# A Strassen down projection with five running sums per output block, and another staging place for the last up tiles

## The chip, the cores and the metric

The kernel runs on one core of one Trainium2 chip. The metric is the device time of one execution in microseconds (us); lower is better. Three executions of the kernel before took 2719.97, 2726.58 and 2727.91 us, median 2726.58. The profiled execution took 2729.51 us; its records span 2727.7 us.

The engines are named as in the profile: PE is TensorE's matmuls (PEld its weight loads), DVE is VectorE, ACT is ScalarE, POOL is GpSimd and SP is SyncE, on which all the transfers spoken of here are issued. Each engine works through its own instructions in a fixed order; semaphores hold an instruction back until what it needs is done.

## The reference

The reference is one inference step of a two-layer decoder over 1024 prompt tokens and 64 sample tokens, which the kernel treats as one matrix of T = 1088 columns. Layer 0 mixes with a state-space model, layer 1 with attention over a cache; each then has the same kind of MLP, and that is the part that matters here:

```python
def sqrelu_mlp(x, w_up, w_down):
    h = jax.nn.relu(x @ w_up)
    return (h * h) @ w_down
...
h = h + sqrelu_mlp(rmsnorm(h, p["norm_mlp"][i]), p["w_up"][i], p["w_down"][i])
```

D_MODEL is 1024 and the hidden width 4096. All is float32.

## The kernel before, in words

**Arithmetic.** A float32 operand is kept as a high and a low part, and one product of two operands is three matmuls (`mm3`, whose matmul is line 209). Making the two parts is `split`: an ACT copy (line 221) and a DVE subtraction (line 222).

**Tiling.** T is cut into four chunks of CN = 272 columns. Activations lie transposed: features on the 128 partitions, tokens along the free axis. A product of 2x2 blocks is done with seven block products in place of eight (Strassen's scheme in Winograd's form). `weight_ops` (lines 390 to 425) loads a raw weight tile, forms the seven weight operands with four POOL instructions (lines 416, 417, 418 and 422) and splits them; `operands` does the same for activations.

**`seven`** (lines 427 to 454) runs the seven products p0 to p6 of one output unit and makes the four quarters c11, c12, c21, c22 from them. Each product goes to one of three pairs of PSUM banks, taken in turn, so p(i+3) cannot start before p(i) has been read. The scheme is: s1 = p0 (ACT copy, line 439); u2 = p1 + s1 (DVE, 441); c11 = p2 + s1; u4 = p3 + u2 (DVE, 445); c22 = p4 + u4; u2 = p4 + u2 (DVE, 449); c12 = p5 + u4; c21 = p6 + u2. In the up stage a product is 24 matmuls, in the down stage 12.

**`mlp`** first runs 16 up tiles (14, 0 to 13, 15). The hidden rows are eight blocks b of two tiles; for b = 0 to 6 `to_hidden` turns a pair of tiles into seven activation operands and stores them in DRAM (`hops`). The rows of block 7 (tiles 14 and 15) are not combined: their four quarters are split in four staging places of `setA` (`hl4`) and stored in `hcnv`, eight stores, two for each quarter. The stores and the loads of the next operands share SP's queue and are chained one after the other (`load_on`, issue on line 526).

**The down stage** (lines 609 to 646) works on an array `H5` that is `setA` seen as two column groups by two halves n by eight output row blocks. For each hidden block b = 0 to 6 and each half d of the output rows it has a *pair* of units, e = 0 and e = 1; while the e = 1 unit of a pair runs, the weight operands of the next pair are made. So there are 28 units in a layer, of 84 matmuls each. `out` adds a quarter into H5. For b = 0 it writes H5 (one DVE instruction, line 627). For b = 1 to 6 it takes a DVE addition of the PSUM bank (line 629) and a POOL addition of s1, u4 or u2 (line 630): seven DVE, one ACT and four POOL instructions in a unit. For b = 1 to 4 POOL also adds the residual that was saved before the MLP (line 646), two instructions in a unit. Two tiles of H5 matter for the start: rows 0 to 3 (d = 0) of the half n = 1, into which c12 and c22 go, lie in the first 1088 words of `setA[1]` and `setA[3]`, and the fourth staging place is the first 1088 words of `setA[1]`. The first staging place is the first 1088 words of `setA[0]`, where c11 and c21 of d = 0 go. For b = 0 and d = 0 the two units run by turns, product by product.

**Block 7** is then multiplied plainly, without the seven products (lines 647 to 666).

**Order.** The program is written in its natural order, and a scheduler (`schedule_with_timeline_sim=True`) fixes the order in which each engine gets its instructions. The order therefore changes where the program does, on every engine.

## Time and profile before

| what | value |
|---|---|
| median of three runs | 2726.58 us (2719.97 to 2727.91) |
| profiled execution | 2729.51 us, span 2727.7 us, mean granted TensorE clock 0.978 |
| busy, whole span | PE 2564.0 us (94%), DVE 1959.2 (72%), ACT 1256.6 (46%), POOL 1213.1 (44%) |
| matmuls of 128 x 272 (line 209, three largest groups) | 15800, of 20369 matmuls in all |
| down-stage additions | line 629 DVE x192, line 630 POOL x192 |

The down stage of layer 0 begins on PE at 843.32 us and block 7 near 1167 us; in layer 1 the same steps lie some 1498 us later (2341.55 us). PE is 94% busy, so the times that matter are the short stretches where it isn't, and what PE waits for there. Busy times of the other engines count only where PE waits for them.

### The profile page before, as it was taken

How to read it: one execution, taken by the hardware profiler on the slowest of the kernel's cores; microseconds unless marked ns; L12 is line 12 of the kernel's file. 1: busy time of each engine (PE TensorE's matmuls, PEld its weight loads, DVE VectorE, ACT ScalarE, POOL GpSimd, SP SyncE). 2: the span in 40 equal slices, each digit the busy share in tenths (PEclk: the TensorE clock that was granted, in tenths of full speed). 3: DMA queues.
4: the chain of work that ended last, by engine and by line, in shares of the span. 5: the costliest groups of instructions: out<-in, count | busy, mean ns of one | idle time of the engine just before them, and what ended most of it. 6: DMA issues, size and time to landing. Idle time of an engine off the chain costs nothing.

```text
span 2727.7 us, 54053 instructions
## 1 busy us (share of the span) xinstructions
PE 2564.0 (94%) x20369; PEld 2392.2 (88%) x20369; DVE 1959.2 (72%) x3406; ACT 1256.6 (46%) x2612; POOL 1213.1 (44%) x1119
## 2 busy tenths in 40 slices
PE   6888899999998999999999999999989999899998
PEld 5777779899998999999889867777989999899998
DVE  8898665988886777794323278886588788677776
ACT  5433444566663222244322367775366665322224
POOL 4576310323321799842310455651032222179984
PEclk8999899999999999999999999999999999999999
DMA  6445352266558567443476889986226656866741
GB/s 200 106 104 146 117 163 76 91 242 243 229 228 324 232 254 277 178 167 102 150 259 222 268 290 308 304 294 218 91 87 244 236 227 234 318 242 244 285 169 67
DMA packets 242283, 561.66 MB, mean 206 GB/s; under 512 B 54053, under 2 KB 129382, under 8 KB 224614
## 3 DMA queue, kind: packets, MB, share of 16 engines
q1 hardware_dynamic: 212646, 548.50, 56.7%
q10 hardware_dynamic: 28864, 8.92, 1.4%
q8 instruction: 161, 2.64, 0.4%
q0 software_dynamic: 512, 0.79, 0.1%
q14 instruction: 100, 0.82, 0.1%
HBM read 386.19 MB, written 171.93 MB: 205 GB/s over the span
## 4 chain that ended last, share of the span: by engine, by line
PE 41%; DVE 18%; POOL 10%; DMA 10%; issue 6%; ACT 4%; SPq 0%; POOLq 0%; ACTq 0%; DVEq 0%
PE banks L209 39%; DMA hops<-plain 5%; DVE rounded L222 5%; POOL plain L630 4%; DVE plain L222 4%; PE banks L1667 1%; POOL plain L416 1%; DMA rounded<-hmid 1%; DVE plain L578 1%; POOL plain L646 1%; ACT plain L221 1%; POOL plain L422 1%; DMA hcnv<-plain 1%; POOL plain L417 1%; DMA plain<-fpast 1%
## 5 line engine op out<-in xcount | busy, mean ns | idle before, releaser
L209 PE MATMUL banks<-rounded 128*128 128x272 f32 (+3 forms) x11168 | 1552.6, 295 | 72.8 <-ACT rounded L221 18.3
L209 PEld LDWEIGHTS banks<-rounded 128*128 128x128 f32 x11168 | 1456.7, 191 | 120.3 <-ACT rounded L221 21.1
L221 ACT ACTIVATE rounded<-plain 128x512 fp32r<-128x512 f32 (+5 forms) x573 | 379.8, 676 | 637.5 <-PE banks L209 449.3
L222 DVE TENSOR_TENSOR rounded<-plain,rounded 128x512 fp32r<-128x512 f32 (+4 forms) x518 | 502.8, 976 | 121.7 <-ACT rounded L221 120.3
L209 PE MATMUL banks<-mlp,rounded 128*128 128x272 f32 x3816 | 516.8, 290 | 12.2 <-DVE plain L627 4.8
L209 PEld LDWEIGHTS banks<-mlp,rounded 128*128 128x128 f32 x3816 | 493.8, 189 | 17.2 <-DVE plain L627 5.3
L416 POOL TENSOR_TENSOR plain<-plain 128x512 f32<-128x512 f32 x60 | 103.9, 1731 | 705.9 <-DVE rounded L222 705.9
L630 POOL TENSOR_TENSOR plain<-plain,flex 128x544 f32<-128x544 f32 x192 | 289.8, 1520 | 37.7 <-DVE plain L629 34.8
L222 DVE TENSOR_TENSOR plain<-plain 128x544 fp32r<-128x544 f32 x212 | 171.1, 820 | 69.9 <-ACT plain L221 69.1
L221 ACT ACTIVATE plain<-plain 128x544 fp32r<-128x544 f32 x212 | 136.7, 650 | 111.6 <-DMA hops<-plain 99.1
L629 DVE TENSOR_TENSOR plain<-banks,plain 128x544 f32<-128x544 f32 x192 | 137.9, 718 | 50.3 <-PE banks L209 46.8
L422 POOL TENSOR_TENSOR plain<-plain 128x512 f32<-128x512 f32 x60 | 98.3, 1639 | 63.0 <-DVE rounded L222 62.6
L209 PE MATMUL banks<-flexr,rounded 128*128 128x272 f32 x816 | 114.5, 290 | 4.0 <-DVE flexr L222 4.0
L209 PE MATMUL banks<-layer 128*32 128x256 f32 (+3 forms) x1152 | 111.9, 368 | 5.5 <-DVE layer L1770 1.7
L579 ACT ACTIVATE plain<-plain 128x544 f32<-128x544 f32 (+1 forms) x136 | 83.2, 613 | 66.0 <-DVE plain L578 65.5
L209 PEld LDWEIGHTS banks<-flexr,rounded 128*128 128x128 f32 x816 | 107.8, 191 | 4.4 <-DVE flexr L222 4.4
L222 POOL TENSOR_TENSOR rounded<-plain,rounded 64x512 fp32r<-64x512 f32 (+2 forms) x55 | 77.9, 1424 | 67.1 <-ACT rounded L221 61.9
L222 POOL TENSOR_TENSOR rounded<-flex,rounded 128x544 fp32r<-128x544 f32 (+7 forms) x100 | 65.9, 668 | 83.7 <-ACT rounded L221 71.0
L578 DVE TENSOR_TENSOR plain<-banks,plain 128x544 f32<-128x544 f32 (+1 forms) x136 | 90.5, 666 | 11.8 <-PE banks L209 11.2
L222 DVE TENSOR_TENSOR rounded<-banks,rounded 128x512 fp32r<-128x512 f32 (+2 forms) x136 | 86.0, 637 | 13.1 <-ACT rounded L221 11.3
L221 ACT ACTIVATE rounded<-banks 128x512 fp32r<-128x512 f32 (+2 forms) x136 | 75.1, 559 | 42.0 <-PE banks L1667 29.3
L418 POOL TENSOR_TENSOR plain<-plain 128x512 f32<-128x512 f32 x60 | 91.7, 1528 | 2.8
(365 smaller groups left out, 3227.0 us busy)
## 6 DMA issues: line engine op xcount, KB each, us to landing
hops<-plain SPq DMA_DIRECT2D x196, 544.0 KB
rounded<-hops SPq DMA_DIRECT2D x66, 1088.0 KB
plain<-in_cache_kT SPq DMA_DIRECT2D x128, 384.0 KB
layer<-in_cache_v SPq DMA_DIRECT2D x128, 384.0 KB
mlp<-hops SPq DMA_DIRECT2D x32, 1088.0 KB
plain<-in_w_up SPq DMA_DIRECT2D x32, 1024.0 KB
plain<-in_w_down SPq DMA_DIRECT2D x28, 1024.0 KB
plain<-in_xT SPq DMA_DIRECT2D x8, 1088.0 KB
```

The source lines that it names most:

```text
L209: PE.matmul(out, a, b, start=first, stop=last)
L221: S.activation(H, src, AF.Copy)
L222: return e.tensor_tensor(L, src, H.bitcast(F32), op=ALU.subtract)
L416: G.tensor_tensor(a22, a21, a22, op=ALU.add)
L417: G.tensor_tensor(a21, a11, a21, op=ALU.subtract)
L418: G.tensor_tensor(a11, a22, a11, op=ALU.subtract)
L422: G.tensor_tensor(a12, a12, a11, op=ALU.subtract)
L578: V.tensor_tensor(x, ps, u, op=ALU.add)
L579: S.activation(x, x, AF.Relu)
L629: V.tensor_tensor(h, ps, h, op=ALU.add)
L630: G.tensor_tensor(h, h, u, op=ALU.add)
L646: G.tensor_tensor(hc, hc, hr[:, m, :], op=ALU.add)
```

## The change

Names: in the lists below `banks` is PSUM, `flex_8251` the area that holds the temporaries, `plain` the area that holds `setA` (so H5) and the raw weights, `rounded` the split operands.

The down stage no longer uses `seven`. The function that runs one product is taken out of it (`products`), and the down stage keeps, for each unit, five sums over all b: the four quarters in H5 and a fifth one, u2 (`sums2`). For b = 0 they are written, and for later b added to:

- p0 goes into c11 and u2, p3 into c12 and c22, p4 into c22 and c21 (two places each); p1 goes into u2, p2 into c11, p5 into c12, p6 into c21.
- A product that goes to two places is copied from PSUM by ACT to a temporary and added to the one place by DVE, straight from PSUM, and from the temporary to the other by POOL (`twice`, and the three lines after p4). For b = 0 the ACT copy writes the first place itself, and DVE's `once` for the following product reads that place as its second operand.
- At b = 6 u2 is added to c22, c12 and c21 on POOL, three instructions in a unit.
- A unit with b = 1 to 5 now has seven DVE, three ACT and three POOL instructions, with b = 6 seven, three and six, and with b = 0 five, three and none. Over both layers POOL additions go from 192 to 168, ACT copies from 56 to 168, DVE additions from 392 to 376.
- `sums2` lies in the first 2176 words of `flex`, and five temporaries of 544 words behind it.

The fourth staging place moves from words 0 to 1087 of `setA[1]` to words 1088 to 2175, which in H5 are rows 4 to 7, so d = 1.

```diff
-    def seven(lhs, rhs, nk, gs, tmp, out):
-
-        s1, u2, u4 = (t[:, gs] for t in tmp)
-
+    def products(lhs, rhs, nk, gs):
         def product(i):
...
+        return product
...
-                hl4 = [hl.p[1], hl.p[0], hl.p[2], setA[1].sub(0, 1088)]
+                hl4 = [hl.p[1], hl.p[0], hl.p[2], setA[1].sub(1088, 1088)]
...
-        small = joined([sq0, rs0])
-        tmps = Ring([small.sub(544 * i, 544) for i in range(6)])
+
+        sums2 = Place(flex.t, 0, SET // 4).at([128, 2, 4, CN])
+        tmps = Ring([Place(flex.t, SET // 4 + 544 * i, SET // 4 + 544 * i + 544) for i in range(5)])
...
-                    def out(m, n, ps, u):
-                        h = H5[:, :, n, 4 * d + 2 * e + m, :]
+                    m0 = 4 * d + 2 * e
+                    c11, c12, c21, c22 = (H5[:, :, n, m0 + m, :] for m in range(2) for n in range(2))
+                    u2 = sums2[:, :, 2 * d + e, :]
...
+                    def twice(a, c, ps):
+
                         if b == 0:
-                            V.tensor_tensor(h, ps, u, op=ALU.add)
+                            S.activation(a, ps, AF.Copy)
                             return
-                        V.tensor_tensor(h, ps, h, op=ALU.add)
-                        G.tensor_tensor(h, h, u, op=ALU.add)
...
+                        t = tmps(sh)
+                        S.activation(t, ps, AF.Copy)
+                        V.tensor_tensor(a, ps, a, op=ALU.add)
+                        G.tensor_tensor(c, c, t, op=ALU.add)
+
+                    def once(a, ps, c=None):
+                        V.tensor_tensor(a, ps, a if c is None or b else c, op=ALU.add)
+
+                    twice(c11, u2, product(0))
+                    yield
+                    once(u2, product(1), c11)
+                    yield
+                    once(c11, product(2))
+                    yield
+                    twice(c12, c22, product(3))
+                    yield
+                    ps = product(4)
+                    once(c22, ps, c12)
+                    if b == 0:
+                        S.activation(c21, ps, AF.Copy)
+                    else:
+                        t = tmps(sh)
+                        S.activation(t, ps, AF.Copy)
+                        G.tensor_tensor(c21, c21, t, op=ALU.add)
+                    yield
+                    if b == 6:
+                        G.tensor_tensor(c22, c22, u2, op=ALU.add)
+                    once(c12, product(5))
+                    yield
+                    once(c21, product(6))
+                    if b == 6:
+                        for c in (c12, c21):
+                            G.tensor_tensor(c, c, u2, op=ALU.add)
+                    yield
```

Below, lines of the changed kernel carry its own numbers: `twice` is lines 634 to 642 (637 the b = 0 copy, 640 the copy, 641 DVE, 642 POOL), `once` is line 645, p4's copy is 658 (b = 0) or 661, POOL's addition to c21 is 662, and the additions of u2 at b = 6 are 665 and 671.

**The start of the down stage.** DVE before, from the first two writes of H5 on (line 627 writes c11, then c22 and later quarters of the d = 0 units; 445 and 449 are u4 and u2; a DMAHW wait is one for a transfer):

```order
L627 TENSOR_TENSOR plain<-banks,flex_8251 128x2x272 [waits DMAHW7_49,DVE_49]
L627 TENSOR_TENSOR plain<-banks,flex_8251 128x2x272 [waits DMAHW0_49]
L445 TENSOR_TENSOR flex_8251<-banks,flex_8251 128x544 [waits PE_49]
L222 TENSOR_TENSOR rounded<-plain,rounded 128x512 [waits Activation_49]
L222 TENSOR_TENSOR rounded<-plain,rounded 128x512 [waits PE_49,Activation_49]
L627 TENSOR_TENSOR plain<-banks,flex_8251 128x2x272 [waits DMAHW0_49,DVE_49]
L449 TENSOR_TENSOR flex_8251<-banks,flex_8251 128x544
```

After, the first writes of H5 are ACT's copies of p0, behind the last splits of the staging, and the first DVE rows are these two pieces:

```order
L637 ACTIVATE plain<-banks 128x2x272 [waits DMAHW7_49]
L637 ACTIVATE plain<-banks 128x2x272 [waits DMAHW0_49,PE_49]
```

```order
L645 TENSOR_TENSOR flex_8251<-banks,plain 128x2x272 [waits PE_49,Activation_49]
L645 TENSOR_TENSOR flex_8251<-banks,plain 128x2x272 [waits DVE_49,PE_49,Activation_49]
L222 TENSOR_TENSOR rounded<-plain,rounded 128x512 [waits Activation_49]
L645 TENSOR_TENSOR plain<-banks,plain 128x2x272 [waits DMAHW7_49,DVE_49,PE_49]
L645 TENSOR_TENSOR plain<-banks,plain 128x2x272 [waits DMAHW0_49,DVE_49,PE_49]
L222 TENSOR_TENSOR rounded<-plain,rounded 128x512 [waits Activation_49]
L222 TENSOR_TENSOR rounded<-plain,rounded 128x512 [waits PE_49,Activation_49]
L645 TENSOR_TENSOR plain<-banks,plain 128x2x272 [waits PE_49]
```

The third line-627 row, which waits for a transfer and stands ahead of line 449, has no counterpart after: the rows that follow c11 there wait for PE and ACT only.

**POOL in a unit that makes weights**, b = 5, d = 0, e = 1. Before, and then after:

```order
L416 TENSOR_TENSOR plain<-plain 128x4x128
L417 TENSOR_TENSOR plain<-plain 128x4x128
L630 TENSOR_TENSOR plain<-plain,flex_8251 128x2x272
L418 TENSOR_TENSOR plain<-plain 128x4x128
L630 TENSOR_TENSOR plain<-plain,flex_8251 128x2x272
L422 TENSOR_TENSOR plain<-plain 128x4x128
```

```order
L642 TENSOR_TENSOR flex_8251<-flex_8251 128x2x272 [waits Activation_49]
L416 TENSOR_TENSOR plain<-plain 128x4x128 [waits DMAHW6_49,DVE_49]
L417 TENSOR_TENSOR plain<-plain 128x4x128 [waits Pool_49]
L418 TENSOR_TENSOR plain<-plain 128x4x128 [waits Pool_49]
L642 TENSOR_TENSOR plain<-plain,flex_8251 128x2x272 [waits Activation_49]
L422 TENSOR_TENSOR plain<-plain 128x4x128 [waits DVE_49,Pool_49]
L662 TENSOR_TENSOR plain<-plain,flex_8251 128x2x272 [waits Activation_49]
```

The addition to u2 now stands ahead of the first weight instruction, and the addition between 417 and 418 is gone.

**DVE in the same unit, after**: each `once` behind a POOL addition waits for POOL, and `twice`'s addition waits for ACT's copy of the same bank. Before, none of the additions to H5 or the temporaries waited for POOL's addition to another quarter of the same unit.

```order
L641 TENSOR_TENSOR plain<-banks,plain 128x2x272 [waits Activation_49]
L645 TENSOR_TENSOR flex_8251<-banks,flex_8251 128x2x272 [waits PE_49,Pool_49]
L645 TENSOR_TENSOR plain<-banks,plain 128x2x272 [waits DVE_49,PE_49]
L222 TENSOR_TENSOR rounded<-plain,rounded 128x512 [waits Activation_49]
L222 TENSOR_TENSOR rounded<-plain,rounded 128x512 [waits PE_49,Activation_49]
L641 TENSOR_TENSOR plain<-banks,plain 128x2x272 [waits Activation_49]
L222 TENSOR_TENSOR rounded<-plain,rounded 128x512 [waits PE_49,Activation_49]
L645 TENSOR_TENSOR plain<-banks,plain 128x2x272 [waits DVE_49,PE_49]
L222 TENSOR_TENSOR rounded<-plain,rounded 128x512 [waits Activation_49]
L645 TENSOR_TENSOR plain<-banks,plain 128x2x272 [waits Pool_49]
```

The three rows with POOL or ACT in their wait (641, 645 on u2 and the last 645, on c22) are the new links; ACT's copy of p4 (line 661) in turn waits for that last DVE row.

More of the change, by code (lines that the diff above doesn't have):

```diff
@@ L437, in product, with seven @@
             return v[:, gs]
+        return product
+    def seven(lhs, rhs, nk, gs, tmp, out):
+        s1, u2, u4 = (t[:, gs] for t in tmp)
+        product = products(lhs, rhs, nk, gs)
         S.activation(s1, product(0), AF.Copy)
@@ L623, in down @@
                 def down(e):
-                    def out(m, n, ps, u):
-                        h = H5[:, :, n, 4 * d + 2 * e + m, :]
+                    m0 = 4 * d + 2 * e
+                    c11, c12, c21, c22 = (H5[:, :, n, m0 + m, :] for m in range(2) for n in range(2))
+                    u2 = sums2[:, :, 2 * d + e, :]
+                    product = products(lambda i, k: (W[i][:, 0, e, k, :], W[i][:, 1, e, k, :]),
+                                       lambda i, g, k: tuple(ops[i][:, k, x, CN * g:CN * g + CN] for x in range(2)),
+                                       2, slice(0, 2))
```

3 lines of the change are left out of this document (removed).

## The prediction

> **What bounds the kernel now.** I read the page first (PE is 94% busy, so only its gaps count), then a table of stretches over the down stage of layer 0. Its columns are length, PE, PEld, DVE, ACT and POOL busy, granted clock, and transfers.
>
> ```profile
> 816.00:884.00 68.00, 56.32 (x412) 55.16 (x411) 42.83 (x61) 26.44 (x45) 12.11 (x8) 0.92 0.88 333
> 884.00:952.00 68.00, 67.05 (x534) 66.61 (x533) 49.99 (x65) 16.36 (x27) 50.14 (x37) 1.00 0.56 217
> 952.00:1020.00 68.00, 63.90 (x497) 62.34 (x496) 50.85 (x63) 16.03 (x27) 63.38 (x47) 1.00 0.66 258
> 1020.00:1088.00 68.00, 65.76 (x516) 64.67 (x516) 51.21 (x65) 16.16 (x27) 65.54 (x49) 1.00 0.70 273
> 1088.00:1156.00 68.00, 67.50 (x531) 66.46 (x530) 54.34 (x66) 16.82 (x27) 57.83 (x40) 1.00 0.50 197
> ```
>
> Two places lose time: the first stretch (PE 56.32 of 68, POOL hardly used), and the third and fourth, where POOL is busy 63.38 and 65.54 of 68. The first, on PE's timeline and then on DVE's, ACT's and SP's, with the last row from the chain of waits:
>
> ```profile
> 843.32 3.27 PE L209 MATMUL banks<-rounded 128*128 128x272 f32 x24 [0.94 <-DVE plain L449]
> 853.52 1.76 PE L209 MATMUL banks<-mlp,rounded 128*128 128x272 f32 x12 [0.93 <-DVE flex L441]
> 857.71 3.09 PE L209 MATMUL banks<-mlp,rounded 128*128 128x272 f32 x12 [2.42 <-DVE plain L627]
> 861.47 4.74 PE L209 MATMUL banks<-rounded 128*128 128x272 f32 x36 [0.67 <-DMA rounded<-hops]
> 872.93 9.24 PE L209 MATMUL banks<-rounded 128*128 128x272 f32 x53 [6.72 <-DVE flex L449]
> 856.95 1.39 DVE L627 TENSOR_TENSOR plain<-banks,flex 128x544 f32<-128x544 f32 x2
> 871.52 0.72 DVE L627 TENSOR_TENSOR plain<-banks,flex 128x544 f32<-128x544 f32 x1 [5.54 <-DMA hcnv<-plain]
> 880.08 0.72 DVE L627 TENSOR_TENSOR plain<-banks,flex 128x544 f32<-128x544 f32 x1 [0.78 <-PE banks L209]
> 848.82 2.29 ACT L221 ACTIVATE plain<-plain 128x544 fp32r<-128x544 f32 x4
> 851.14 4.43 SPq L526 DMA_DIRECT2D hcnv<-plain  x2
> 857.16 6.60 SPq L526 DMA_DIRECT2D hcnv<-plain  x5
> 860.04 11.39 DMA hcnv<-plain
> 2371.28 10.16 PE L209 MATMUL banks<-rounded 128*128 128x272 f32 x60 [6.79 <-DVE flex L449]
> ```
>
> PE stands still for 6.72 us because DVE's write of c22 at 871.52 waits for a store of `hcnv` that lands at 871.43: the fourth staging place is where it writes. Layer 1 shows the same gap (6.79). The clean rate of PE comes from a run without gaps and the row behind it:
>
> ```profile
> 1024.08 9.18 PE L209 MATMUL banks<-rounded 128*128 128x272 f32 x72
> 1033.09 1.16 PE L209 MATMUL banks<-mlp,rounded 128*128 128x272 f32 x8
> ```
>
> 72 matmuls take 1033.09 - 1024.08 = 9.01 us, 0.1251 each: 1.50 us a product, 10.5 a unit, 21.02 a pair. The first pair of the stage starts at 843.32 and its last quarter is evicted from 880.08, 36.8 us later where 21.0 would do. The other losses I read off DVE's additions for p1 of the e = 0 units, one pair apart where I name pairs:
>
> ```profile
> 904.15 0.72 DVE L441 TENSOR_TENSOR flex<-banks,flex 128x544 f32<-128x544 f32 x1 [0.30 <-PE banks L209]
> 1085.43 0.71 DVE L441 TENSOR_TENSOR flex<-banks,flex 128x544 f32<-128x544 f32 x1
> 1107.30 0.71 DVE L441 TENSOR_TENSOR flex<-banks,flex 128x544 f32<-128x544 f32 x1
> ```
>
> The eight pairs of b = 1 to 4 take 181.28 us, 22.66 each, so 1.64 over the clean 21.02. The first pair of b = 5, which has no residual additions, takes 21.87: 0.85 over. So POOL matters in b = 1 to 4, and what is left in b = 5 is waiting between engines.
>
> **What the move of the staging place is worth.** It removes the wait of 871.52: c12 and c22 of d = 0 no longer touch a staged place. What stays is the first staging place, under c11 and c21. Its new first writer is ACT's copy of p0, behind ACT's four staging splits, which end at 848.82 + 2.29 = 851.1. The store of its high half was issued at 851.14 and both halves had landed by 856.95, where DVE wrote c11. In the changed order DVE does its staging splits without line 441 between them, so I put the second store at about 853.1 and its landing at 855.5 (nearest row: the second store went on SP before 855.57 = 851.14 + 4.43, and c11 was free 1.4 us later). Then p1 of e = 1, which needs p0's bank, starts near 854.3, and p2 near 856.2, in place of 853.52 and 857.71, and nothing later in the pair waits for a store: of the 84 x 2 = 168 matmuls the remaining 120 take 15.0 us, and 871.2 is the end of the pair. The slow clock after a gap (0.92 in this stretch; the 53 matmuls at 872.93 would take 6.63 at 0.1251 and took 9.24, 2.6 more) may stay: 873.8. Against 880.08 that is 6.3 us a layer; I take 6.2, with 2 (ACT's copies are held as long as DVE's line 627 was, and p4 is late) to 9 (no slow clock either) as bounds.
>
> The Trainium skill, "TensorE: Matmul & The Clock Gate", part 1, says that a window without matmuls drops PE's clock and that it takes some time of work to come back. The trace agrees in the slow 53 matmuls after the 6.72 us gap. By it the shorter gaps after the change would cost less of this than 2.6.
>
> **What the five sums cost in a steady unit.** First the throughput. Groups by line, and one e = 1 unit of b = 5 on POOL, DVE and ACT:
>
> ```profile
> L630 POOL TENSOR_TENSOR plain<-plain,flex 128x544 f32<-128x544 f32 x192 | 289.8, 1520 | 37.7 <-DVE plain L629 34.8
> L629 DVE TENSOR_TENSOR plain<-banks,plain 128x544 f32<-128x544 f32 x192 | 137.9, 718 | 50.3 <-PE banks L209 46.8
> L439 ACT ACTIVATE flex<-banks 128x544 f32<-128x544 f32 x25 | 15.3, 612 | 7.1 <-PE banks L209 5.4 <-ACT rounded L221 1.7
> 1094.11 1.29 POOL L416 TENSOR_TENSOR plain<-plain 128x512 f32<-128x512 f32 x1 [0.63 <-DVE rounded L222]
> 1095.48 1.29 POOL L417 TENSOR_TENSOR plain<-plain 128x512 f32<-128x512 f32 x1
> 1096.73 1.81 POOL L630 TENSOR_TENSOR plain<-plain,flex 128x544 f32<-128x544 f32 x1
> 1098.51 1.75 POOL L418 TENSOR_TENSOR plain<-plain 128x512 f32<-128x512 f32 x1
> 1100.21 1.38 POOL L630 TENSOR_TENSOR plain<-plain,flex 128x544 f32<-128x544 f32 x1
> 1101.55 1.74 POOL L422 TENSOR_TENSOR plain<-plain 128x512 f32<-128x512 f32 x1
> 1103.24 3.59 POOL L630 TENSOR_TENSOR plain<-plain,flex 128x544 f32<-128x544 f32 x2
> 1103.76 0.71 DVE L629 TENSOR_TENSOR plain<-banks,plain 128x544 f32<-128x544 f32 x1
> 1104.39 2.99 DVE L222 TENSOR_TENSOR rounded<-plain,rounded 128x512 fp32r<-128x512 f32 x2
> 1103.86 0.61 ACT L439 ACTIVATE flex<-banks 128x544 f32<-128x544 f32 x1
> ```
>
> A pair had 8 POOL additions and has 6: 2 x 1.4 = 2.8 us of POOL fall away (1.38 and 1.81 are the ends). POOL was busy some 63.38/68 x 22.66 = 21.1 to 65.54/68 x 22.66 = 21.8 us of a pair; 18.3 to 19.0 is left, under PE's 21.02. As a throughput bound POOL is gone. ACT gains four copies of 0.61 a pair, some 2.4 us on an engine that was 16.16 busy of 68; DVE keeps 14 additions of 0.72.
>
> Then the waits. The new chain in an e = 1 unit is p3, ACT's copy, POOL's addition to c22, DVE's addition of p4, ACT's copy of p4, POOL's addition to c21, DVE's addition of p6; POOL also does the weight instructions there, in the order u2, 416, 417, 418, c22, 422, c21. I lay it on the clock of the quoted unit:
>
> - POOL adds to u2 from 1093.6 (p0's copy, in the place of line 439) to 1095.0, and 416, 417, 418 follow, to 1099.3 (1.29, 1.29 and 1.75).
> - c22 += p3's copy ends between 1100.7 (1.38) and 1101.1 (1.81). DVE, in its order, first finishes the splits ahead of it; c22 += p4 ends near 1102.9 to 1103.2.
> - 422 ends at 1102.4 to 1102.9, so ACT's copy of p4 stands behind ACT's split of its result and ends at 1103.7 to 1104.3; only then is p4's bank free. The changed PE order starts the next unit with p1 instead of p0, and p1 waits for a weight split at 1102.2 to 1102.5.
> - c21 += p4's copy ends at 1105.1 to 1106.5 and DVE's c21 += p6 is done at 1105.8 to 1107.2; the unit's last bank pair would be wanted at about 1104.4.
>
> So PE loses 1.3 to 2.5 us at each such unit; the e = 0 units make no weights, POOL has 3 x 1.4 us of work in 10.5 there, and I cost them at nothing (cover: the third bank pair; without it each POOL link is 1.4). I take 1.8, nearer the low end, since of the POOL rows above 416, 417 and one 630 stand at 1.29 to 1.38. Against before:
>
> - b = 1 to 4: 8 x (1.8 - 1.64) = +1.3 (bounds -2.7 and +6.9).
> - b = 5: 1.2 a pair, without residual additions, against 0.85 in the first pair: two pairs, +0.7 (-0.5 to +2).
> - b = 6: three more POOL additions a unit, two of e = 0 ahead of 416 and two between 417 and 422: 422 moves back by up to 4 x 1.4 us, c21 with it, and there POOL does 12 x 1.4 plus the 6.1 us of the weight rows, 22.9, against 21.02 in one pair: +2 to +3 with what waits behind it, and the last pair has no weights: +2.4 (0 to +5).
> - b = 0 pairs: POOL-free; the copies replace additions of about the same length: 0.
>
> Sum +4.4 a layer (bounds -3 and +14).
>
> At one place the Trainium skill speaks against this change: "PSUM — Partial Sum Buffer", section "PSUM bank collisions raise a hardware error", says that two engines must not access the same bank at once, so copy and addition of one product run one behind the other. The changed order agrees (641 waits for Activation, 661 for DVE); by rows that is 0.61 + 0.72 = 1.3 us in place of 0.72 until a bank is free, and it is in the layout above.
>
> "SBUF — State Buffer", section "Who interferes with whom", says that a DVE instruction with both inputs in SBUF contends with POOL. The trace agrees: the two DVE splits at 1104.39 take 2.99 while POOL adds, and DVE's additions from PSUM stay at 0.72. By it fewer POOL instructions would also shorten splits, a gain that I leave in the lower bound.
>
> **The sum.** Per layer -6.2 + 4.4 = -1.8, over two layers -3.6 us. The profiled execution was 2729.5, 2.9 over the median 2726.6; a difference of -3.6 puts the changed kernel's profile at 2725.9 and its median at **2723 us**, the number that I forecast. That is 0.13%, and about 0.3% (8.2 us) is what a measurement of this kernel can tell from none: no change. This case's own range is 2716 to 2733.
>
> **The rivals.**
>
> - *The waits fit under three bank pairs* (low ends): steady -1 a layer, transition -6.2: -14.4, **2712**. For it: POOL gets 2.8 us a pair back and was the busiest there. Against: b = 5 has free POOL now and still loses 0.85.
> - *POOL was all of the steady loss*: each of the eight pairs comes down to 21.5, -9.3 a layer, b = 6 +1, transition -6.2: -29, **2698**. Against it: the chain above.
> - *The chain through POOL becomes the bound, slower*: in the unit that makes weights DVE waits for POOL's c21 where before nothing of DVE's waited there. Upper ends: +7 + 2 + 3 = +12 a layer, transition only -3: +18, **2745**. It decides once DVE's addition of p6 ends over 1.2 us after its bank is wanted, about 1105.6 on the clock above. For it: POOL's rows of 1.75 to 1.81 beside DVE's splits, and the weight chain starting behind the u2 addition.
> - *The staging move does nothing*: ACT's copy of p0 waits for the first store as long as DVE's c11 did (856.95), and the loads that SP issues between the stores then set p1 and p2. Transition 0, steady +4.4: +8.8, **2735**. For it: the gap 2.42 ended by line 627 was a wait for that store. Against: 6.72 of the gaps was the last store.
>
> **How the numbers follow.** Forecast 0.36; waits fit 0.25; POOL all of it 0.08; POOL chain 0.20; staging nothing 0.11. Faster by over 0.3% (under 2718.4): the 0.33 of the two fast cases and 0.03 of the forecast's: 0.36. Slower (over 2734.8): 0.20 and about half of the last, 0.06: 0.26. The same: 0.38. The range reaches over most of the cases on both sides: below 2704 lies most of 2698's 0.08, above 2745 half of 2745's 0.20, together under 0.2.
>
> **What would show it.** Right for the move: no gap of 6 us ended by DVE near 865 to 873, no DVE or ACT wait for `hcnv` of over 3 us, the first pair done by 875. Right for the sums: pairs of b = 1 to 4 near 22.8 us, POOL busy under 60 of 68, and PE's remaining gaps in e = 1 units ended by DVE or ACT, behind POOL's 642 and 662. Wrong: pairs under 22 us (the waits are hidden) or over 23.3 (they bound); a first pair that still ends near 880; or a new gap elsewhere, such as block 7 waiting for the last POOL additions of u2.

## The result and the profile after

The changed kernel takes 2760.8 us (median of four, 2751.83 to 2763.18) against 2726.58 (2719.97 to 2727.91): a ratio of 1.0128, 95% interval 1.0112 to 1.0143. It is slower by 34 us, where 2723 was forecast and 2745 was the upper end of the range. The same two places tell where the time went. The table of stretches of layer 0 after, with the columns of the one shown before:

```profile
816.00:884.00 68.00, 60.83 (x472) 60.40 (x471) 43.25 (x60) 31.15 (x53) 12.15 (x8) 0.95 0.88 333
884.00:952.00 68.00, 63.91 (x496) 62.18 (x496) 45.19 (x60) 22.61 (x39) 45.74 (x36) 1.00 0.67 255
952.00:1020.00 68.00, 61.25 (x468) 58.85 (x467) 48.03 (x60) 22.42 (x38) 54.06 (x41) 1.00 0.59 233
1020.00:1088.00 68.00, 60.87 (x465) 58.49 (x463) 47.42 (x58) 21.20 (x36) 50.38 (x38) 1.00 0.56 216
1088.00:1156.00 68.00, 62.10 (x482) 60.44 (x481) 44.47 (x60) 21.75 (x36) 46.58 (x33) 1.00 0.56 223
```

PE gains in the first stretch (60.83 busy where it was 56.32) and loses in all that follow (60.87 in the fourth, where it was 65.76). POOL is not full any more (50.38, it was 65.54), and yet PE stands still more. In the first stretch, the rows of the first pair on PE, those on DVE and ACT that end its long gap, and the last eviction on DVE:

```profile
842.52 3.27 PE L209 MATMUL banks<-rounded 128*128 128x272 f32 x24 [1.18 <-DVE plain L451]
853.28 3.08 PE L209 MATMUL banks<-mlp,rounded 128*128 128x272 f32 x12 [5.99 <-ACT plain L637]
862.31 10.66 PE L209 MATMUL banks<-rounded 128*128 128x272 f32 x84
847.89 4.13 DVE L222 TENSOR_TENSOR plain<-plain 128x544 fp32r<-128x544 f32 x3
852.06 0.66 ACT L221 ACTIVATE plain<-plain 128x544 fp32r<-128x544 f32 x1 [3.13 <-DVE plain L222]
852.62 0.61 ACT L637 ACTIVATE plain<-banks 128x544 f32<-128x544 f32 x1
871.52 0.72 DVE L645 TENSOR_TENSOR plain<-banks,plain 128x544 f32<-128x544 f32 x1 [0.77 <-PE banks L209]
```

The gap of 6.72 us in the middle of the pair is gone; one of 5.99 has come at p1 of e = 1, behind ACT's copy of p0 (637). That copy does not stand idle for a store: it follows ACT's last staging split (852.06) at once, and this split had waited 3.13 us for DVE's staging splits. The second copy of p0 does wait for the first store, 1.35 us up to 854.58, while PE is at work. The last quarter is evicted at 871.52, where it was 880.08.

I count pairs by PE's own order: a layer's stage is 14 times 168 matmuls, and a pair's time is the start of its first matmul to that of the next pair's. In us, as the mean over both layers:

| pairs | before | after |
|---|---|---|
| the first (b = 0, d = 0) | 36.65 | 28.82 |
| b = 1 to 4, sum of eight | 178.72 | 194.78 |
| b = 5, sum of two | 43.62 | 48.08 |
| b = 6, sum of two | 43.00 | 49.22 |
| stage, 14 pairs | 322.98 | 341.91 |

The stage is 18.9 us longer in a layer: 7.8 won in the first pair, 26.7 lost in the twelve of b = 1 to 6. Twice 18.9 is 37.9; the spans differ by 2760.7 - 2727.7 = 33.0. The rest, some 5 us, lies outside the two stages, most of it between them (the changed kernel is 17.1 us behind where the first ends and 13.0 where the second starts); I did not follow that further.

One unit that makes weights, at the end of b = 4, on PE, then the rows of POOL, ACT and DVE that end in its gaps:

```profile
1086.88 1.27 PE L209 MATMUL banks<-rounded 128*128 128x272 f32 x8 [0.22 <-DVE rounded L222]
1089.20 1.77 PE L209 MATMUL banks<-rounded 128*128 128x272 f32 x12 [1.05 <-ACT flex L661]
1092.42 1.77 PE L209 MATMUL banks<-rounded 128*128 128x272 f32 x12 [1.46 <-DVE plain L645]
1094.03 6.16 PE L209 MATMUL banks<-mlp,rounded 128*128 128x272 f32 x48
1084.45 1.82 POOL L642 TENSOR_TENSOR plain<-plain,flex 128x544 f32<-128x544 f32 x1
1086.24 1.73 POOL L422 TENSOR_TENSOR plain<-plain 128x512 f32<-128x512 f32 x1
1087.93 2.38 POOL L684 TENSOR_TENSOR plain<-plain,rounded 128x272 f32<-128x272 f32 x2
1090.28 1.33 POOL L662 TENSOR_TENSOR plain<-plain,flex 128x544 f32<-128x544 f32 x1
1088.00 0.63 ACT L221 ACTIVATE rounded<-plain 128x512 fp32r<-128x512 f32 x1 [1.31 <-POOL plain L422]
1088.54 0.60 ACT L661 ACTIVATE flex<-banks 128x544 f32<-128x544 f32 x1
1086.74 0.71 DVE L645 TENSOR_TENSOR plain<-banks,plain 128x544 f32<-128x544 f32 x1
1091.64 0.72 DVE L645 TENSOR_TENSOR plain<-banks,plain 128x544 f32<-128x544 f32 x1 [1.96 <-POOL plain L662]
```

Three gaps follow each other: PE waits for a weight split inside the next unit's first product, at the second product for the bank of p4, at the third for that of p6. DVE has added p4 to c22 by 1087.45, but ACT's copy of p4 stands behind ACT's split of what POOL's 422 makes, and starts at 1088.54. POOL then has two residual additions (684) ahead of c21, and DVE adds p6 at 1091.64. Between the last matmul before the first gap (52 of them from 1079.98, so about 1086.5) and 1092.42 PE runs 8 + 12 matmuls, 2.5 us of work in 5.9: 3.4 us lost at one unit. The three gaps are one delay and not three: by its own work PE would have wanted p6's bank near 1089.0, and DVE frees it at 1092.36, so without the first two gaps PE would have waited longer at the third.

### The profile page after: what moved, and what is told of

Its sections match the earlier page's. It is cut to its first block, busy times and chain, and to the rows that moved or that the text cites. A ratio compares the mean times of both kernels' runs of the same rounds, so it can differ in the third digit from the quotient of the medians.

```text
span 2760.7 us, 54265 instructions
## 1 busy us (share of the span) xinstructions
PE 2571.8 (93%) x20369; PEld 2390.6 (87%) x20369; DVE 1947.5 (71%) x3390; ACT 1320.9 (48%) x2724; POOL 1173.5 (43%) x1095
## 4 chain that ended last, share of the span: by engine, by line
PE 43%; DVE 16%; POOL 11%; DMA 9%; issue 6%; ACT 4%; SPq 0%; POOLq 0%; ACTq 0%; DVEq 0%
PE banks L209 41%; DVE rounded L222 5%; DMA hops<-plain 5%; DVE plain L222 3%; DVE plain L645 2%; POOL plain L662 2%; POOL plain L684 1%; POOL plain L416 1%; PE banks L1705 1%; POOL plain L417 1%; DMA rounded<-hmid 1%; POOL plain L642 1%; ACT plain L221 1%; DVE plain L580 1%; POOL plain L418 1%
## 5 line engine op out<-in xcount | busy, mean ns | idle before, releaser
L222 DVE TENSOR_TENSOR rounded<-plain,rounded 128x512 fp32r<-128x512 f32 (+4 forms) x518 | 488.8, 949 | 102.2 <-ACT rounded L221 96.6
L645 DVE TENSOR_TENSOR plain<-banks,plain 128x544 f32<-128x544 f32 x224 | 160.9, 720 | 124.1 <-POOL plain L662 59.3
L640 ACT ACTIVATE flex<-banks 128x544 f32<-128x544 f32 x96 | 59.2, 617 | 136.9 <-PE banks L209 132.0
```

The lines of the kernel that those rows point to most:

```text
L222: return e.tensor_tensor(L, src, H.bitcast(F32), op=ALU.subtract)
L640: S.activation(t, ps, AF.Copy)
L645: V.tensor_tensor(a, ps, a if c is None or b else c, op=ALU.add)
```

## The experiments

In the same sessions the kernel before took 2723 to 2726 us. "Pairs" are means over b = 1 to 4 and over b = 5 and 6, counted as above.

**Theory A at first: the move is worth the first pair, the rest is the new chain behind p4.** The rival of the split was that the five sums themselves shorten the first pair.

*The move alone* (before, one line changed):

```diff
-                hl4 = [hl.p[1], hl.p[0], hl.p[2], setA[1].sub(0, 1088)]
+                hl4 = [hl.p[1], hl.p[0], hl.p[2], setA[1].sub(1088, 1088)]
```

> The kernel before with the fourth staging place moved and nothing else (the down stage still makes the four quarters with seven). Theory A (the move is worth what the first pair showed, 36.6 us down to 28.8, 7.8 a layer, and all of the loss is in the five sums): first pair 29 to 30 us in each layer, the other pairs as before (21.0 to 23.5), some 13 to 15 us less than before, 2711 to 2714 us. Rival S (the shorter first pair came from the five sums, whose first writes are ACT's copies, so the move alone brings nothing): first pair still about 36.6, time 2724 to 2730 us.

Measured 2709.83 us against 2725.31, ratio 0.9947 (0.993 to 0.9965). The first pair takes 28.52 and 26.89 us, the others are as before (22.42 and 21.65). Its first pair on PE:

```profile
849.77 1.76 PE L209 MATMUL banks<-mlp,rounded 128*128 128x272 f32 x12 [0.94 <-DVE flex L441]
854.76 3.09 PE L209 MATMUL banks<-mlp,rounded 128*128 128x272 f32 x12 [3.23 <-DVE plain L627]
857.65 12.08 PE L209 MATMUL banks<-rounded 128*128 128x272 f32 x84
```

One gap is left, of 3.23 us, ended by DVE's first write of H5 (627), which follows DVE's splits and line 445 without idle time; no row waits for a store. The 6.72 us are gone. Theory A holds here, the gain a little over its range; rival S falls.

*The five sums alone* (the changed kernel with the old place, the same line the other way).

> The changed kernel with the fourth staging place put back where it was (five sums kept). Theory A: the first pair goes back to 35 to 37 us, the other pairs stay near 24.5, and the time is 13 to 16 us over the changed kernel, 2773 to 2777 us. Rival S (the sums shorten the first pair themselves): first pair under 32, time within 5 us of the changed kernel, 2756 to 2766 us.

Measured 2783.58 us, 22.8 over the changed kernel, beyond what either expected. First pair 38.15 and 38.64, the other pairs as in the change (24.30 and 24.33). The old gap is back and stands behind the new one:

```profile
855.73 3.09 PE L209 MATMUL banks<-mlp,rounded 128*128 128x272 f32 x12 [7.13 <-ACT plain L637]
872.86 10.77 PE L209 MATMUL banks<-rounded 128*128 128x272 f32 x72 [6.34 <-ACT plain L637]
```

Now both are ended by ACT's copy (637). The two parts do not simply add: the move is worth 15.5 us without the sums and 22.8 with them, and the sums cost 58.3 (2783.58 - 2725.31) with the old place and 51.0 (2760.8 - 2709.8) with the new one.

*p4's places exchanged* (in the changed kernel, b = 1 to 6), so that DVE adds p4 to c21 and POOL the copy to c22. With `twice`, ACT's copy of p4 also comes ahead of DVE's addition, where it came behind it in the change; a later run tests that alone:

```diff
-                    once(c22, ps, c12)
...
-                        t = tmps(sh)
-                        S.activation(t, ps, AF.Copy)
-                        G.tensor_tensor(c21, c21, t, op=ALU.add)
+                        twice(c21, c22, ps)
```

> The changed kernel with the two places of p4 exchanged for b = 1 to 6: DVE adds p4 to c21 straight from PSUM, and POOL adds the copy to c22, so c22 is added to by POOL alone and neither DVE's addition of p4 nor that of p6 waits for POOL; the numbers of instructions on each engine stay the same. Theory A (the loss is the chain POOL to DVE to ACT behind p4, which frees two banks late): of the 3.5 us lost in a pair the two gaps behind p4's copy (1.3) and behind c21 (1.7) go, pairs come from 24.5 to 21.6 to 22.4, time 2700 to 2716 us. Rival L (the loss is the load: 112 more ACT copies and two reads of a bank, whatever waits for what): pairs stay at 24 to 25, time 2755 to 2765 us. Rival P (the loss is the order in which PE gets the products, p1 ahead of p0): it follows the order alone, 2740 to 2765 us if the order stays as it is.

Measured 2752.85 us, pairs 23.76 and 23.60: 8 us won where theory A said 45 to 60. Rival L's time was nearly met, and it lies in rival P's range, which names PE's order of the products. What speaks against P as the cause is the run with p3 alone exchanged (below): in its trace p0 is the first product of every unit of layer 0 from b = 1 on, and the pairs still take 23.2 to 23.7 us.

*Four bank pairs in place of three* in the changed kernel's down stage:

> The changed kernel with four pairs of PSUM banks in place of three in the down stage (banks 6 and 7 as the fourth), the five sums and their chains unchanged. Theory A (a bank is free too late by 1.3 to 1.7 us, which one more product of 1.5 us in between covers): pairs at 21.3 to 22.5 us, time 2698 to 2718 us. Rival L (engines are loaded, or POOL's chain itself is longer than a unit): pairs at 23.5 or more, 2745 us or more.

Measured 2793.0 us, 32 slower than the change, pairs 24.57 and 26.32. Theory A in this form falls. The scheduler gave another order, and in it DVE's addition of p4 stands behind two weight splits (rows of DVE, ACT and PE):

```profile
1011.80 2.90 DVE L222 TENSOR_TENSOR rounded<-plain,rounded 128x512 fp32r<-128x512 f32 x2
1014.63 1.34 DVE L645 TENSOR_TENSOR plain<-banks,plain 128x544 f32<-128x544 f32 x2
1015.37 0.62 ACT L661 ACTIVATE flex<-banks 128x544 f32<-128x544 f32 x1 [3.88 <-DVE plain L645]
1016.12 6.26 PE L209 MATMUL banks<-rounded 128*128 128x272 f32 x36 [2.41 <-ACT flex L661]
```

PE's wait for the copy grew from 1.05 to 2.41 us. What the fourth pair would do with the order held is not told by this run.

**Theory B: banks that two engines read one behind the other. Rival K: the links through POOL.** Two runs let DVE add the temporary instead of reading the bank a second time, the second with p0's and p4's places exchanged as well:

```diff
-                        V.tensor_tensor(a, ps, a, op=ALU.add)
+                        V.tensor_tensor(a, t, a, op=ALU.add)
```

> The changed kernel, with DVE adding the temporary instead of reading the bank a second time, for the three products that go to two places (p0, p3, p4; b = 1 to 6): the bank is read by ACT's copy alone, and DVE's addition then has both inputs in SBUF. The links through POOL stay (u2 before p1, c22 before p4's addition, c21 before p6). Theory B (after exchanging p4's places and after a fourth bank pair have fallen short: PE waits for banks that two engines read one behind the other, each behind weight splits in its own queue): the gaps behind p0, p3 and p4 shrink and what is left is p1's and p6's wait for POOL, pairs 22.3 to 23.3 us in place of 24.5, time 2728 to 2744 us. Rival K (the links through POOL are the cost, whichever engine reads the bank): pairs stay at 24 to 25 us, 2755 to 2765 us. Rival C (DVE with two SBUF inputs loses to POOL what the bank gains): DVE's addition takes 1 us or more instead of 0.72, pairs 24 us or more.

> As the run before it, and the places exchanged so that POOL's sums are not waited for soon: p4's copy goes to c21 by DVE and to c22 by POOL (which alone adds to c22), p0's copy to u2 by DVE and to c11 by POOL (which DVE needs for p2, one product later). Each bank is then read by one engine once, and one link through POOL is left. Theory B: pairs 21.3 to 22.3 us, time 2700 to 2715 us, about as fast as the kernel before with the moved staging place alone. Rival K: both causes taken together, the same numbers; it and theory B differ in the run before this and in the one after. Rival L (load: ACT's copies and the additions as such): pairs at 24 us.

Measured 2826.67 and 2804.46 us, pairs 26.42 and 27.81, then 25.05 and 27.29: far slower, both. DVE in a unit that makes weights, in the second of them, with two rows of POOL:

```profile
1035.32 1.90 DVE L641 TENSOR_TENSOR flex<-flex 128x544 f32<-128x544 f32 x1
1037.96 0.71 DVE L645 TENSOR_TENSOR plain<-banks,plain 128x544 f32<-128x544 f32 x1
1040.38 3.61 DVE L641 TENSOR_TENSOR plain<-flex,plain 128x544 f32<-128x544 f32 x2
1053.44 0.78 DVE L641 TENSOR_TENSOR plain<-flex,plain 128x544 f32<-128x544 f32 x1
1055.46 0.72 DVE L641 TENSOR_TENSOR plain<-flex,plain 128x544 f32<-128x544 f32 x1 [1.24 <-ACT flex L640]
1035.27 1.37 POOL L642 TENSOR_TENSOR plain<-plain,flex 128x544 f32<-128x544 f32 x1 [1.03 <-ACT flex L640]
1055.57 1.83 POOL L642 TENSOR_TENSOR plain<-plain,flex 128x544 f32<-128x544 f32 x1 [1.93 <-ACT flex L640]
```

An addition of 544 words takes 0.71 with one input in PSUM. With both inputs in SBUF it takes 1.8 to 1.9 where POOL's instruction began first: the one at 1035.32 ends 0.6 us after POOL's, which began at 1035.27. Where DVE begins first (1055.46) it takes 0.72, and POOL's is the longer one, 1.83 in place of 1.37. Rival C holds (1 us or more for the addition, 24 us or more for a pair). Reading the bank twice was the cheaper way.

*p0's and p4's places exchanged, DVE still adding from the bank:*

```diff
-                    twice(c11, u2, product(0))
+                    twice(*((u2, c11) if b else (c11, u2)), product(0))
```

and p4 as above.

> The changed kernel with the places of p4 and of p0 exchanged as in the run before, but DVE still adding from the PSUM bank behind ACT's copy: the links through POOL are gone (but c11 before p2), the two reads of a bank stay. Theory B: pairs 23.3 to 24.3 us, 2742 to 2755 us, little better than with p4 alone exchanged (2752.9). Rival K (links through POOL, of which u2's before p1 was still there when p4 was exchanged): pairs 21.5 to 22.5 us, 2700 to 2718 us.

Measured 2701.88 us, ratio 0.9919 (0.9903 to 0.9936), pairs 21.76 and 21.95. Two reads of each bank are still there, so theory B falls and rival K holds. The same count of instructions on each engine, so load (rival L) falls too. PE's waits from 890 to 1170 us, in total, times and longest, of the change and then of this kernel:

```profile
PE banks L209 <- DVE plain L645: 10.2, 10, 1.5
PE banks L209 <- ACT flex L661: 8.8, 8, 1.4
PE banks L209 <- DVE rounded L222: 4.2, 10, 1.3
```

```profile
PE banks L209 <- DVE flex L641: 2.3, 8, 0.4
PE banks L209 <- ACT rounded L221: 0.9, 1, 0.9
PE banks L209 <- DVE plain L645: 0.8, 1, 0.8
```

*The move with four bank pairs, on the scheme of before:*

> The kernel before with the moved staging place and four pairs of PSUM banks in the down stage. There POOL is busy some 21.4 of 22.7 us in a pair of b = 1 to 4. Theory B with POOL as the bound of those pairs: a fourth pair brings nothing in b = 1 to 4 (22.3 to 23.5 us) and at most 0.6 us a pair in b = 5 and 6; 2704 to 2714 us (the moved place alone: 2709.8). Rival O (the fourth pair slowed the changed kernel down because the scheduler then sets another order, whatever the scheme): over 2718 us here too.

Measured 2703.39 us, 0.992 (0.9903 to 0.9936). Pairs of b = 1 to 4 22.40 (as with three), of b = 5 and 6 21.14 (21.65 with three). The time is 0.6 us under theory B's range, and rival O falls. In b = 1 to 4 POOL stays the bound of the scheme of before:

```profile
1020.00:1088.00 68.00, 65.17 (x515) 64.29 (x514) 51.89 (x64) 16.87 (x29) 65.78 (x49) 1.00 0.74 292
```

**Which link.** c22 between p3 and p4 and u2 between p0 and p1 leave one product of time; c21 between p4 and p6 leaves two.

*p0 alone exchanged* (the u2 link gone):

> The changed kernel with the places of p0 alone exchanged (b = 1 to 6): DVE adds p0 to u2 from the bank, POOL the copy to c11, which DVE needs for p2. The link through POOL that has one product of time (u2 between p0 and p1) becomes one with two (c11 between p0 and p2); c22 between p3 and p4 (one product) and c21 between p4 and p6 (two) stay as in the change. So far: none exchanged 2760.8, p4 exchanged 2752.9, both 2701.9. Theory K1 (a link with one product of time in between costs, one with two does not; and either one of the two short links is enough to hold the unit up): pairs 23.5 to 24.3 us, 2738 to 2756 us. Rival K0 (the u2 link, first in the unit and ahead of the weights, is nearly all of the cost): pairs 21.5 to 22.2, 2698 to 2715 us.

Measured 2771.3 us, 10 more than the change, pairs 24.88 and 24.00. Both theories missed, K0 by far. The gaps of 1.05 behind p4's copy and 1.46 behind c21 stand in it to the hundredth, and between 890 and 1170 us PE also waits 7.7 us, in three gaps of up to 2.6, for DVE's addition of p0 to u2 (641), which the change does not have:

```profile
1097.30 1.77 PE L209 MATMUL banks<-rounded 128*128 128x272 f32 x12 [1.05 <-ACT flex L661]
1100.53 1.77 PE L209 MATMUL banks<-rounded 128*128 128x272 f32 x12 [1.46 <-DVE plain L645]
```

*p3 alone exchanged* (DVE adds p3 to c22, POOL to c12, so the c22 link is gone):

```diff
-                    twice(c12, c22, product(3))
+                    twice(*((c22, c12) if b else (c12, c22)), product(3))
```

> The changed kernel with the places of p3 alone exchanged (b = 1 to 6): DVE adds p3 to c22 from the bank, POOL the copy to c12, which DVE needs for p5, two products later. Of the short links only u2 stays; p4 is as in the change (DVE, then ACT's copy, then POOL's c21). Theory K1: about what exchanging p4 gave (2752.9), which took the same short link away: 2740 to 2757 us. Rival K2 (what costs is the long chain behind p4, DVE's addition, ACT's copy and POOL's c21): no better than the change, 2756 to 2765 us. Rival K3 (the c22 link is nearly all): under 2715 us.

Measured 2741.57 us, pairs 23.23 and 23.65: 19 us won, within K1.

*p0 and p3 exchanged* (no short link left, p4 as in the change):

> The changed kernel with the places of p0 and p3 exchanged (b = 1 to 6): no link through POOL with one product of time is left, three with two products are (c11, c12, c21). POOL gets its additions in the same places of its queue as in the change. Theory K1: pairs 21.4 to 22.2 us, as with p0 and p4 exchanged, 2698 to 2712 us. Rival K2 (p4's chain by ACT's copy and POOL's c21): pairs over 23 us, 2735 us or more.

Measured 2726.74 us, pairs 22.81 and 22.74. 34 us won, between K1 (2698 to 2712) and K2 (2735 or more): with both short links gone a good half of the 59 us that p0 and p4 exchanged win is won, and the long chain behind p4, with two products of time, is not free. In it PE still waits at c21:

```profile
1096.42 3.26 PE L209 MATMUL banks<-rounded 128*128 128x272 f32 x24 [0.26 <-ACT flex L661]
1100.95 1.77 PE L209 MATMUL banks<-rounded 128*128 128x272 f32 x12 [1.27 <-DVE plain L645]
```

*p0 and p4 exchanged, with four bank pairs:*

> The kernel with p0 and p4 exchanged (2701.9) and four pairs of PSUM banks in the down stage. Theory K1: what a pair still loses there (0.5 to 0.6 us behind DVE's second reading of p0's bank) is covered by the fourth pair, pairs 21.0 to 21.6 us, 2690 to 2702 us. Rival O (a fourth pair lets the scheduler set an order in which DVE's additions stand behind weight splits, as in the changed kernel, where it cost 32 us): over 2706 us.

Measured 2695.27 us, 0.9898 (0.9873 to 0.9924), pairs 21.47 and 21.27. The fastest of all, under both kernels of the case. It lies in K1's range, and rival O falls: with the short links gone the fourth pair helps, by 0.3 and 0.7 us a pair.

**What stayed open, in three runs.**

*The copy of p4 ahead of DVE's addition* (the changed kernel, two lines in the other order):

```diff
-                    once(c22, ps, c12)
...
                         S.activation(t, ps, AF.Copy)
+                        once(c22, ps)
                         G.tensor_tensor(c21, c21, t, op=ALU.add)
```

> The changed kernel with ACT's copy of p4 ahead of DVE's addition to c22 (b = 1 to 6); nothing else differs. In the change the copy waits for DVE's addition, then stands behind ACT's split of what 422 makes, and only then POOL adds to c21. Theory K2 (this chain behind p4, to the bank and to c21, makes two of the three gaps in a pair): the gap behind the copy (1.05 us) goes, the one behind c21 (1.46) shrinks by at least 1, pairs 22.3 to 23.3 us, 2725 to 2742 us. Rival K3 (the links as such, u2 and c22, which are untouched): pairs 24 us or more, 2752 to 2765 us.

Measured 2748.15 us, pairs 23.51 and 23.92, between the two. The gap behind 661 is gone from PE's waits, but other gaps came in its place:

```profile
PE banks L209 <- ACT rounded L221: 5.4, 8, 0.8
PE banks L209 <- DVE plain L641: 4.9, 10, 0.7
PE banks L209 <- DVE plain L645: 4.5, 8, 0.9
```

So taking ACT's wait away brought 13 us in the order that came with it, and is not the one cause.

*The residual additions left out:*

> The changed kernel with the residual additions of the down stage left out (POOL's line 684, two in a unit of b = 1 to 4), so the residual of blocks b = 1 to 4 is missing from the output. Theory R (the two residual additions that stand ahead of POOL's c21 addition are why the pairs of b = 1 to 4 lose 3.5 us and not the 1.8 that was forecast from a unit of b = 5): those pairs 22.5 to 23.5 us, b = 5 and 6 as before, 2738 to 2750 us. Rival K2 (the chain behind p4 is the same without them): pairs of b = 1 to 4 still 24 to 25, 2752 to 2762 us.

Measured 2741.42 us. The pairs come to a flat 23.5 from b = 2 to the end of b = 5. The second pair of b = 5 and those of b = 6 stay; the first of b = 5, whose gaps lie behind the last unit of b = 4, falls from 24.55 to 23.5 with the others. PE in such a unit, to be held against the one shown above:

```profile
1080.29 1.27 PE L209 MATMUL banks<-rounded 128*128 128x272 f32 x8 [0.21 <-DVE rounded L222]
1082.61 1.78 PE L209 MATMUL banks<-rounded 128*128 128x272 f32 x12 [1.04 <-ACT flex L661]
1084.80 1.77 PE L209 MATMUL banks<-rounded 128*128 128x272 f32 x12 [0.41 <-DVE plain L645]
```

The gap behind c21 falls from 1.46 to 0.41, the two others don't move. Theory R holds: 1.1 us a pair is the residual additions that stand ahead of POOL's c21.

*p4 exchanged and the u2 addition left out:*

> The kernel with p4 exchanged (2752.9), and POOL's addition of p0's copy to u2 left out for b = 1 to 6, so that p1's addition waits for nothing of POOL; the output lacks p0 in three quarters for those b. Theory K0 (with p4's links gone, the link of u2 alone holds the unit at 24.3 us): pairs 21.3 to 22.2 us, about 2698 to 2712 us, as with p0 and p4 exchanged, though POOL has one addition less in a unit. Rival D (p4's exchange itself, with DVE's second read of p4 behind weight splits, holds it there): pairs 23.5 us or more, 2740 us or more.

Measured 2716.49 us, pairs 22.59 and 21.65. Leaving out this link, and POOL's work with it, wins 36 of the 51 us that separate p4 alone from p0 and p4. K0 is the nearer, but the time is 4 us over its range, and so are the pairs of b = 1 to 4.

**What follows.** The loss goes with the links through POOL. They lie beside each other and not in a row, so what one is worth depends on the rest: u2's is worth nothing (-10) with p4's chain in place, 15 us with c22's gone (2741.57 to 2726.74), and 36 (left out) to 51 (exchanged) with p4's links gone. Not every link is itself a wait: in the unit shown the one that waits is DVE's addition of p6, 1.96 us for POOL's c21, while POOL had finished c22 by 1086.27 and DVE was at a split until 1086.82. By what way the link of c22 costs the 19 us that exchanging p3 wins is not shown. What can't be told apart: each of these kernels also got its own order from the scheduler, and no run held the order and took a link away.

## Why the prediction was wrong

- **What bounds the kernel before**: right. The store of the fourth staging place was the 6.72 us, and POOL the bound of b = 1 to 4; with the move and four bank pairs those pairs stay at 22.4 with POOL at 65.78 of 68.
- **The move**: right, and a little under. Forecast 6.2 us a layer, measured 7.8 in the first pair, and 15.5 for both layers by itself. p1 of e = 1 was put at 854.3 and started at 853.28. What I had it wait for, the first store, is not what held it: DVE's and ACT's staging splits did. That p2 started at 856.17, where 856.2 was forecast, is luck. The term that was off is the slow clock: I kept 2.6 us behind p2, and in the changed kernel it shows almost only in the 12 matmuls from 853.28, which last until the next row at 856.17, 2.89 us where 1.5 would do. I had expected less of it after a shorter gap, and the runs do not show that: with the move alone, after a gap of 3.23 us, the 12 matmuls from 854.76 take 2.89 us and the 84 behind them 11.92 where 10.5 would do, 2.8 us lost (granted clock 0.50 to 0.53 up to 861), against 1.5 after 5.99 us in the changed kernel. The Trainium skill ("TensorE: Matmul & The Clock Gate", part 1) says that the window which sets the clock runs freely, so that the moment of the change varies. The traces agree in so far as the loss does not follow the length of the gap.
- **POOL as a throughput bound is gone**: right (54.06 and 50.38 busy where under 60 was given).
- **The steady units, the step that failed**: +4.4 us a layer forecast, bounds -3 and +14, and 26.7 measured. By blocks, b = 1 to 4 +1.3 forecast and +16.1 measured, b = 5 +0.7 and +4.5, b = 6 +2.4 and +6.2. The layout itself was nearly right: it had every link, it put ACT's copy of p4 behind ACT's split of 422, and DVE's addition of p6 1.4 to 2.8 us after its bank was wanted (1105.8 to 1107.2 against 1104.4; the 1.3 to 2.5 that I wrote is a little less than that). What failed is the size of "so PE loses 1.3 to 2.5 us at each such unit", of which I took 1.8 for b = 1 to 4 and 1.2 for b = 5. Three things in the sum were wrong.
  1. *The residual additions were not laid in.* The unit was one of b = 5. In b = 1 to 4 two residual additions stand in POOL's queue ahead of c21. Leaving them out gives 1.1 us a pair back, 8.7 a layer (194.78 to 186.12 in b = 1 to 4) of the 16.1.
  2. *I took the low end.* The pair behind the first unit of b = 5, without residuals, takes 23.52 us, 2.5 over the clean 21.02, and with the residual additions left out b = 2 to 4 lose the same: near the top of the range, where I took 1.8 and 1.2. Over b = 1 to 4 that is 3.6 us (186.12 / 8 is 2.25 over 21.02, less the 1.8, eight times).
  3. *The loss of before was read too high.* I took 1.64 a pair from DVE's additions for p1, which themselves wait; by PE's order the pairs of b = 1 to 4 take 178.72 / 8, 1.32 over the clean time. That is 2.6 us.
  These three make up the difference in b = 1 to 4, 14.8 us. The three gaps of PE are not a fourth: they share one delay, which the end of the chain sets. What b = 6 lost beyond the forecast (6.2 against 2.4) no run takes apart.
- **"The e = 0 units make no weights, and I cost them at nothing"**: not what failed. In the unit from 1094.03 PE runs 48 + 36 + 48 matmuls with no gap.
- **The rivals**: the one that ends on the other side, POOL's chain as the bound, had the place and the mechanism, and 2745 for its price; its chance of 0.20 was too low. Its price held the move at 3 us a layer and the sums at +12, where 7.8 and 26.7 were measured. The staging rival fell; its sign, the gap of 2.42 us before, was no wait for a store either, as line 627 at 856.95 follows line 445 (from 856.31) without idle time. Neither of the two faster cases came.
- **The two reads of a bank**: not what cost here. With p0 and p4 exchanged they are all still there at 21.8 us a pair, and the kernel that reads each bank once is slower. The rule of the Trainium skill that I weighed against the change ("PSUM — Partial Sum Buffer", "PSUM bank collisions raise a hardware error") orders the two reads, and the traces agree (ACT's copy of p4 at 1088.54 comes behind DVE's addition, which ends at 1087.45); it pointed at the wrong cost. The other, on DVE and POOL in SBUF ("SBUF — State Buffer", "Who interferes with whom"), bears out: 1.90 us behind an addition of POOL, 0.72 where DVE began first.

## What to carry to other kernels

A running sum that two engines write in turn is a wait of the one for the other's whole queue. Give each sum to one engine where that can be, and put the copy's addition on the sum that is wanted last: two lines that exchange places were worth 59 us here, more than the change itself cost. When a chain is laid by hand, lay it in the fullest of the stages it stands for, with all that stands in each queue, and take the middle of what it gives unless a row speaks for an end.

## What the runs showed that I had not expected

- A DVE addition of 128 x 544 with both inputs in SBUF takes 1.8 to 1.9 us where POOL's instruction began just before it, against 0.72 where DVE began first and 0.71 with one input in PSUM. The kernel that frees the banks early by way of SBUF took 66 us more (2826.67 against 2760.8).
- DVE's staging splits, 4.13 us for three from 847.89 on, and not a store, held the first pair of the changed kernel.
- A fourth pair of PSUM banks made one kernel 32 us slower and two others 6 to 7 us faster, with the same products: with more banks the scheduler set another order, and in the slower one two weight splits came to stand ahead of the addition that frees a bank.
